# State space branch on one core: the bias difference of the decays and the scaling of the results on ScalarE, and the state step for four heads in one instruction

## The chip, the cores and the metric

The kernel runs on one core of a Trainium2 chip. The time is the device time of one execution in microseconds (us). The core's engines work side by side, each through its own list of instructions in order: TensorE (PE, matmuls and transposes; its weight loads are listed as PEld), VectorE (DVE), ScalarE (ACT), GpSimd (POOL, which here mostly issues transfers) and SyncE (SP, which issues transfers of weights). An engine waits when the next instruction in its own list needs something that is not there yet, and all that stands behind that instruction waits too.

## The reference

The kernel computes two transformer-like blocks on 512 tokens in fp32. The change lies in one branch of the second block, a state space branch: 8 groups of 4 heads, sequences cut in chunks of 128 tokens, run forwards and backwards. Cut to what matters:

```python
def segsum_exp(a):
    T = a.shape[-1]
    cs = jnp.cumsum(a, axis=-1)
    diff = cs[..., :, None] - cs[..., None, :]
    tri = jnp.asarray(np.tril(np.ones((T, T), dtype=bool)))
    return jnp.where(tri, jnp.exp(jnp.where(tri, diff, 0.0)), 0.0)

def ssd_chunked(x, dt, A, Bm, Cm):
    ...
    CB = jnp.einsum('bclgn,bcsgn->bcgls', Cc, Bc)
    Wd = CB[:, :, :, None] * segsum_exp(adt)
    y_diag = jnp.einsum('bcgrls,bcsgrp->bclgrp', Wd, xdt)
    ...
    def step(carry, inp):
        st, dec = inp
        return carry * dec[..., None, None] + st, carry
    ...

def ssd_branch(z, xbc, dt_raw, conv_w, conv_b, dt_bias, a_log, d_skip, norm_g):
    xbc = jax.nn.silu(depthwise_conv_centred(xbc, conv_w, conv_b))
    ...
    y_fwd = ssd_chunked(xs, dt[:, :, 0], A[0], Bm, Cm)
    y_bwd = fl(ssd_chunked(fl(xs), fl(dt[:, :, 1]), A[1], fl(Bm), fl(Cm)))
    y = y_fwd + y_bwd + d_skip[:, None] * xs
    y = y.reshape(b, l, D_INNER) * jax.nn.silu(z)
    yg = y.reshape(b, l, SSD_GROUPS, D_INNER // SSD_GROUPS)
    yg = yg * lax.rsqrt(jnp.mean(yg * yg, axis=-1, keepdims=True) + EPS)
    return yg.reshape(b, l, D_INNER) * norm_g
```

Three places of it are touched: the exponents inside `segsum_exp` (forward and backward decays of a chunk are put into one 128x128 matrix per head), `step`, and the product with the `rsqrt`.

## The kernel before, in words

All projections are fp32 products made of three PE passes: `mm3` (L457 to L459) multiplies high and low halves. A projection matmul is 128x128 by 128x512; eight input blocks times three passes, 24 matmuls, fill one of the three wide PSUM buffers (`psm`), which ACT and DVE then empty. Smaller results go through five buffers `pss`. A framework with a scheduler decides in which order each engine's instructions are listed: it plays the program through a timeline of its own and picks what it thinks is ready. So a change of a few lines can reorder the lists around it.

The state space stage works through groups g = 0 to 7. Its names and lines:

- `feats`: two projections of the next group, each emptied by `conv`: ACT L1253 (first tap, with bias) and DVE L1257 (four more taps, read from PSUM), then ACT L1259 (Silu). A `psm` buffer is free after both.
- `turn`: PE transposes the features (L1302, L1303), ACT copies them out (L1304, L1305).
- `first`: PE L1343 makes C·B (`cb`) for four chunks, DVE L1346 takes its diagonal, `step` makes the states (DVE L1310 weights x, PE L1312 multiplies, then ACT L1315 for the first chunk or DVE L1319 for the later ones), and `decays` makes the four 128x512 decay matrices of a group: a POOL transfer (L1327) brings the running sums of all four heads and both directions from DRAM (`aD`) to the 1024-word buffer `ab`, DVE L1329 adds the difference `dlt` of the two directions' biases to the backward half, DVE L1330 copies the forward half over it where the mask says so, ACT L1332 takes four Exp of 128x128 with a bias for each head, DVE L1333 multiplies by `cb`.
- `gate`: for even g, the gate projection with Silu on ACT (L1292).
- `second`: PE L1368/L1370 and DVE L1375/L1376 add the states' part, PE L1381 multiplies the decays by x, DVE L1382 and L1383 finish the chunk and ACT L1384 squares and sums it. L1384 is the last reader of that chunk's `ab`; there are four of them, so the next group's transfer of the same chunk follows it.
- `third`: DVE L510 and POOL L506 make the reciprocal root of the sum (`rr`), DVE L1392 scales the four chunks by it, PE L1394 transposes them, ACT L468 and DVE L469 split them into high and low.
- `ssd_out`: output projections, added up by ACT L623 and DVE L625.

Weights come through SP, and ACT L165 and DVE L167 split them into halves; these two run all the time. Exp, Silu and Ln need different function tables on ACT: an ACT_TABLE_LOAD stands in ACT's list wherever the table changes.

Of the kernel before, what the change touches and what calls it, by code (L numbers as in the profile page):

```python
# [12 lines left out]
AF = mybir.ActivationFunctionType  # L13
ALU = mybir.AluOpType
# [4 lines left out]
P = 128  # L19
# [38 lines left out]
def vw(ap, off, dims):  # L58

    return bass.AP(tensor=ap.tensor, offset=ap.offset + off, ap=[list(ap.ap[0])] + [list(x) for x in dims])  # L60


def dr(ap, off, dims):
    return bass.AP(tensor=ap.tensor, offset=ap.offset + off, ap=[list(x) for x in dims])
# [182 lines left out]
def body(ctx, tc, I, out, dbg=None, stop=None):  # L247
    nc = tc.nc
# [14 lines left out]
    def PS():  # L263
        return ps_s.tile([P, 512], F32, tag="s", name="pss")
# [125 lines left out]
    def colof(nm, k):  # L390
        c = col[nm] + k
        return COL[:, c:c + 1]
# [11 lines left out]
    ps = PS()  # L404
# [42 lines left out]
    def uk(k):  # L447
        if k < 4:
            return UAh[:, k], UAl[:, k]
        return st["UBh"][:, k - 4], st["UBl"][:, k - 4]  # L450
# [10 lines left out]
    def split(dst, src, scale=None):  # L461

        hi, lo = dst
        if scale is None:
            nc.scalar.activation(out=hi, in_=src, func=AF.Copy)  # L465
            nc.vector.tensor_tensor(out=lo, in0=src, in1=hi.bitcast(F32), op=ALU.subtract)  # L466
        else:
            nc.scalar.activation(out=hi, in_=src, func=AF.Copy, scale=scale)  # L468
            nc.vector.scalar_tensor_tensor(out=lo, in0=src, scalar=scale, in1=hi.bitcast(F32), op0=ALU.mult, op1=ALU.subtract)  # L469
# [39 lines left out]
    def rstd4(ss, n):  # L509
        nc.vector.tensor_scalar(out=ss, in0=ss, scalar1=1.0 / n, scalar2=EPS, op0=ALU.mult, op1=ALU.add)  # L510
        return inv_sqrt(ss, 4)
# [248 lines left out]
    o = 0  # L760
# [6 lines left out]
    ps = PS()  # L767
# [362 lines left out]
    for k in range(8 * NT + AHEAD + DELAY):  # L1130
# [3 lines left out]
        q = k - AHEAD - DELAY  # L1134
# [55 lines left out]
    def tok64(tag):  # L1190
        return wk.get(tag, 256).rearrange("p (c h) -> p c h", c=4)

    dtk, nb, dec, wst, ea = (tok64(n) for n in ("dtk", "nb", "dec", "wst", "ea"))
    dlt = wk.get("dlt", 128).rearrange("p (c h) -> p c h", c=4)
# [66 lines left out]
    def bc64(ap):  # L1261

        return vw(ap, 0, [list(ap.ap[1]), [0, 64]])

    h4 = lambda ap: ap.rearrange("p (h d) -> p h d", h=4)

    class Group:
# [39 lines left out]
        def step(s, di, c, prev):  # L1307
            xw = wk.get("xw", 256, 2)
            o = di * 32 + s.hs
            nc.vector.tensor_tensor(out=h4(xw), in0=h4(s.x[:, c]), in1=bc64(wst[:, c, o:o + 4]), op=ALU.mult)  # L1310
            ps = PS()
            nc.tensor.matmul(ps[:, 0:256], s.Bt[:, c], xw, start=True, stop=True)  # L1312
            S_ = wk.get(f"S{di}", 256, 3)
            if prev is None:
                nc.scalar.activation(out=S_, in_=ps[:, 0:256], func=AF.Copy)  # L1315
            else:
                for q in range(4):
                    sl = slice(q * 64, (q + 1) * 64)
                    nc.vector.scalar_tensor_tensor(out=S_[:, sl], in0=prev[:, sl], scalar=dec[:, c, o + q:o + q + 1],  # L1319
                                                   in1=ps[:, sl], op0=ALU.mult, op1=ALU.add)  # L1320
            return S_

        def decays(s, c):

            g, hs = s.g, s.hs
            ab = s.ab[c] = wk.get("ab", 1024, 4)
            nc.gpsimd.dma_start(ab.rearrange("p (d l) -> p d l", d=8), dr(aD, g * 8 * 512 + c * P, [[0, P], [512, 8], [1, P]]))  # L1327
            fw, T = h4(ab[:, 0:512]), h4(ab[:, 512:1024])
            nc.vector.tensor_tensor(out=T, in0=T, in1=vw(dlt[:, c, hs:hs + 4], 0, [[1, 4], [0, P]]), op=ALU.add)  # L1329
            nc.vector.copy_predicated(T, vw(masks, 7 * P, [[0, 4], [1, P]]), fw)  # L1330
            for q in range(4):
                nc.scalar.activation(out=T[:, q], in_=T[:, q], func=AF.Exp, bias=nb[:, c, hs + q:hs + q + 1])  # L1332
            nc.vector.tensor_tensor(out=T, in0=T, in1=vw(s.cb, c * P, [[0, 4], [1, P]]), op=ALU.mult)  # L1333
# [52 lines left out]
        def third(s):  # L1386

            z, g = s.z, s.g
            r = rstd4(s.ss, 256)
            pts = [PS(), PS()]  # L1390
            for c in range(4):
                nc.vector.tensor_scalar(out=z[:, c], in0=z[:, c], scalar1=r[:, c:c + 1], scalar2=None, op0=ALU.mult)  # L1392
                for n in range(2):
                    nc.tensor.transpose(pts[n][:, c * P:(c + 1) * P], z[:, c, n * P:(n + 1) * P], ident)  # L1394
            for n in range(2):
                split(uk((2 * g + n) % 4), pts[n], colof("ssd_norm_2", 2 * g + n))
# [302 lines left out]
```

## Time and profile before

| | us |
|---|---|
| time, median of 3 runs (lowest to highest) | 2580.79 (2578.79 to 2582.44) |
| time of the profiled execution | 2581.83 |
| its span in the profile | 2580.1 |
| PE busy in the span | 2504.9 |
| DVE busy | 1714.5 |
| ACT busy | 1220.2 |
| the state space stage, from 1340 to 1800 | 460.0 |

The span runs from the first to the last recorded instruction of the profiled execution. Busy time of different engines overlaps. The stage's boundaries are rounded to 20 us; its two ends also hold a little of the work before and after it.

### The profile page before, as it was taken

To read this page: it belongs to the slowest core of one execution; us is meant where nothing else is said; L and a number is where in the kernel's file an instruction comes from. 1 tells how busy PE (TensorE), PEld (TensorE's weight loads), DVE (VectorE), ACT (ScalarE), POOL (GpSimd) and SP (SyncE) were. 2 spreads that over 40 slices of the span, in tenths; PEclk is the share of its full clock that TensorE was granted. 3 is DMA by queue.
4 is the path that set the end of the run, shared out by engine and by line. 5 is a ranking of instruction groups with operands and counts; after the bars stand their busy time and mean duration, and the time that the engine had idled before them with its cause. 6 is when DMAs were issued, how large, how long until landed. Compare 5 with 4: busy or idle time off the path is not lost. (4 is left out here: it accounts for less than half of the span.)

```text
span 2580.1 us, 33650 instructions
## 1 busy us (share of the span) xinstructions
PE 2504.9 (97%) x12848; PEld 2088.2 (81%) x12848; DVE 1714.5 (66%) x3048; ACT 1220.2 (47%) x2181; POOL 183.5 (7%) x199
## 2 busy tenths in 40 slices
PE   8999999999999989999999999998999999999998
PEld 7888888778888768877888788787887789878877
DVE  5566567775566657577477788887555466487674
ACT  6333345443476554444356554563455436444342
POOL 1100220000201030000121100010000000100000
PEclk9999999999999989999999999998999999999999
DMA  5521235333232133453334333352221233243441
GB/s 175 162 66 61 87 115 169 125 108 129 82 96 89 63 97 113 140 179 98 102 109 125 106 104 109 104 148 77 73 67 40 84 113 123 82 147 104 141 139 58
DMA packets 202001, 278.11 MB, mean 108 GB/s; under 512 B 10800, under 2 KB 127776, under 8 KB 201840
## 3 DMA queue, kind: packets, MB, share of 16 engines
q1 hardware_dynamic: 190352, 236.29, 29.4%
q0 software_dynamic: 10192, 34.96, 5.0%
q10 hardware_dynamic: 1296, 4.72, 0.5%
q8 instruction: 101, 1.65, 0.3%
q14 instruction: 60, 0.49, 0.1%
HBM read 271.56 MB, written 9.61 MB: 109 GB/s over the span
## 5 line engine op out<-in xcount | busy, mean ns | idle before, releaser
L458 PE MATMUL psm<-XTl,hl 128*128 128x512 f32 (+1 forms) x1400 | 537.3, 384 | 7.8 <-DVE XTl L466 7.8
L457 PE MATMUL psm<-XTh,hl 128*128 128x512 f32 (+1 forms) x1400 | 534.5, 382 | 5.9 <-ACT XTh L465 5.1
L459 PE MATMUL psm<-XTh,hl 128*128 128x512 f32 (+1 forms) x1400 | 533.3, 382 | 0.0
L165 ACT ACTIVATE hl<-raw 128x1024 fp32r<-128x1024 f32 x303 | 319.3, 1056 | 313.9 <-PE psm L459 132.6
L167 DVE TENSOR_TENSOR hl<-raw,hl 128x1024 fp32r<-128x1024 f32 x287 | 352.7, 1233 | 149.0 <-ACT hl L165 147.9
L458 PEld LDWEIGHTS psm<-XTl,hl 128*128 128x128 f32 x1400 | 266.3, 190 | 56.9 <-DVE XTl L466 8.6
L457 PEld LDWEIGHTS psm<-XTh,hl 128*128 128x128 f32 x1400 | 265.9, 190 | 55.7 <-ACT XTh L465 6.1
L459 PEld LDWEIGHTS psm<-XTh,hl 128*128 128x128 f32 x1400 | 266.3, 190 | 48.5
L457 PE MATMUL psm<-hl,XTh 128*128 128x512 f32 (+1 forms) x640 | 231.1, 362 | 4.4 <-ACT XTh L465 3.3
L458 PE MATMUL psm<-hl,XTh 128*128 128x512 f32 (+1 forms) x640 | 229.9, 359 | 0.1
L459 PE MATMUL psm<-hl,XTl 128*128 128x512 f32 (+1 forms) x640 | 229.1, 358 | 0.0
L457 PE MATMUL psm<-hl,UAh 128*128 128x512 f32 x368 | 148.6, 405 | 4.9 <-DVE ACC L625 1.5
L458 PE MATMUL psm<-hl,UAh 128*128 128x512 f32 x368 | 144.9, 395 | 0.0
L459 PE MATMUL psm<-hl,UAl 128*128 128x512 f32 x368 | 143.7, 396 | 0.0
L457 PEld LDWEIGHTS psm<-hl,XTh 128*128 128x128 f32 x640 | 122.3, 191 | 21.8 <-ACT XTh L465 3.7
L458 PEld LDWEIGHTS psm<-hl,XTh 128*128 128x128 f32 x640 | 122.2, 191 | 16.6 <-issue 0.5
L459 PEld LDWEIGHTS psm<-hl,XTl 128*128 128x128 f32 x640 | 122.3, 191 | 15.9 <-issue 0.5
L671 ACT ACTIVATE WK<-psm 128x512 f32<-128x512 f32 x66 | 39.5, 598 | 160.8 <-PE psm L459 160.8
L457 PE MATMUL psm<-hl,UBh 128*128 128x512 f32 (+1 forms) x240 | 93.5, 391 | 1.1 <-ACT UBh L468 0.8
L459 PE MATMUL psm<-hl,UBl 128*128 128x512 f32 (+1 forms) x248 | 94.3, 388 | 0.0
L1257 DVE SCALAR_TENSOR_TENSOR WS<-psm,CW,WS 128x511 f32<-128x511 f32 (+1 forms) x120 | 87.5, 740 | 8.7 <-ACT WS L1253 8.4
L458 PE MATMUL psm<-hl,UBh 128*128 128x512 f32 (+1 forms) x240 | 92.2, 386 | 0.0
(481 smaller groups left out, 4839.2 us busy)
## 6 DMA issues: line engine op xcount, KB each, us to landing
raw<-in_mlp_w_down_dram SPq DMA_DIRECT2D x76, 512.0 KB, 3.3
raw<-in_mlp_w_up_dram SPq DMA_DIRECT2D x64, 512.0 KB, 3.9
raw<-in_w_in_dram SPq DMA_DIRECT2D x60, 512.0 KB, 3.7
raw<-in_w_down_dram SPq DMA_DIRECT2D x38, 512.0 KB, 3.9
WS<-aD POOLq DMA_DIRECT2D x32, 512.0 KB, 5.9
raw<-in_w_up_dram SPq DMA_DIRECT2D x32, 512.0 KB, 3.7
raw<-in_w_in_dram SPq DMA_DIRECT2D x33, 256.0 KB, 3.2
raw<-in_a_w_in_dram SPq DMA_DIRECT2D x16, 512.0 KB, 4.9
```

Of the source, the lines that this page charges most:

```text
L165: s.nc.scalar.activation(out=h, in_=r, func=AF.Copy)
L167: eng.tensor_tensor(out=l, in0=r, in1=h.bitcast(F32), op=ALU.subtract)
L457: nc.tensor.matmul(ps, a[0], b[0], start=first, stop=False, skip_group_check=partial)
L458: nc.tensor.matmul(ps, a[0], b[1], start=False, stop=False, skip_group_check=partial)
L459: nc.tensor.matmul(ps, a[1], b[0], start=False, stop=last, skip_group_check=partial)
L671: nc.scalar.activation(out=rl, in_=ps, func=AF.Relu)
L1257: nc.vector.scalar_tensor_tensor(out=dst[:, o0:o1], in0=ps[:, o0 + d:o1 + d], scalar=cw(j), in1=dst[:, o0:o1], op0=ALU.mult, op1=ALU.add)
```

## The change

Line numbers up to 1314 stay; behind the step they are smaller by one or two. In the changed kernel the step is L1317 and L1318, the transfer L1325, the bias difference L1328, the masked copy L1329, the Exp L1331, the diagonal of `cb` L1345, the values L1380 to L1382, the square L1383 and the scaling L1391.

- `step`, three states in four: four DVE instructions 128x64 that multiply the previous state by the head's decay and add the matmul's result (L1319) become one DVE multiplication 128x256 with the four decays broadcast (L1317, which does not read the matmul's result) and one DVE addition 128x256 from PSUM (L1318).
- `decays`: one DVE addition 128x512 (L1329) becomes four ACT Identity 128x128 (L1328), each with the head's difference as a bias per partition.
- `third`: four DVE scalings 128x256 (L1392) become four ACT Copy with the scale read per partition (L1391).

```diff
--- before.py
+++ after.py
@@ -1314,10 +1314,8 @@
             if prev is None:
                 nc.scalar.activation(out=S_, in_=ps[:, 0:256], func=AF.Copy)
             else:
-                for q in range(4):
-                    sl = slice(q * 64, (q + 1) * 64)
-                    nc.vector.scalar_tensor_tensor(out=S_[:, sl], in0=prev[:, sl], scalar=dec[:, c, o + q:o + q + 1],
-                                                   in1=ps[:, sl], op0=ALU.mult, op1=ALU.add)
+                nc.vector.tensor_tensor(out=h4(S_), in0=h4(prev), in1=bc64(dec[:, c, o:o + 4]), op=ALU.mult)
+                nc.vector.tensor_tensor(out=S_, in0=ps[:, 0:256], in1=S_, op=ALU.add)
             return S_
 
         def decays(s, c):
@@ -1326,7 +1324,8 @@
             ab = s.ab[c] = wk.get("ab", 1024, 4)
             nc.gpsimd.dma_start(ab.rearrange("p (d l) -> p d l", d=8), dr(aD, g * 8 * 512 + c * P, [[0, P], [512, 8], [1, P]]))
             fw, T = h4(ab[:, 0:512]), h4(ab[:, 512:1024])
-            nc.vector.tensor_tensor(out=T, in0=T, in1=vw(dlt[:, c, hs:hs + 4], 0, [[1, 4], [0, P]]), op=ALU.add)
+            for q in range(4):
+                nc.scalar.activation(out=T[:, q], in_=T[:, q], func=AF.Identity, bias=dlt[:, c, hs + q:hs + q + 1])
             nc.vector.copy_predicated(T, vw(masks, 7 * P, [[0, 4], [1, P]]), fw)
             for q in range(4):
                 nc.scalar.activation(out=T[:, q], in_=T[:, q], func=AF.Exp, bias=nb[:, c, hs + q:hs + q + 1])
@@ -1389,7 +1388,7 @@
             r = rstd4(s.ss, 256)
             pts = [PS(), PS()]
             for c in range(4):
-                nc.vector.tensor_scalar(out=z[:, c], in0=z[:, c], scalar1=r[:, c:c + 1], scalar2=None, op0=ALU.mult)
+                nc.scalar.activation(out=z[:, c], in_=z[:, c], func=AF.Copy, scale=r[:, c:c + 1])
                 for n in range(2):
                     nc.tensor.transpose(pts[n][:, c * P:(c + 1) * P], z[:, c, n * P:(n + 1) * P], ident)
             for n in range(2):
```

The scheduler's lists change with it inside the state space stage; POOL's and SP's lists keep their order. ACT's list holds 58 table loads after, 56 before. Three places follow.

ACT at the start of group 0, before, from the table load of L1234 (the end of the preparation of the decay biases) to L1245, an Exp of a `pss` buffer that DVE L1246 reads after it and that `cb` waits for:

```order
L1234 ACTIVATE WS<-WS 128x256
L1292 ACT_TABLE_LOAD
L1292 ACTIVATE h<-psm 128x512
L1332 ACT_TABLE_LOAD
L1332 ACTIVATE WS<-WS 128x128 x4
L165 ACTIVATE hl<-raw 128x1024
L1332 ACTIVATE WS<-WS 128x128 x7
L1245 ACTIVATE WS<-pss 128x256
```

The same place in the changed kernel:

```order
L1234 ACTIVATE WS<-WS 128x256
L1328 ACTIVATE WS<-WS 128x128 x8
L1292 ACT_TABLE_LOAD
L1292 ACTIVATE h<-psm 128x512
L1328 ACTIVATE WS<-WS 128x128 x4
L1331 ACT_TABLE_LOAD
L1331 ACTIVATE WS<-WS 128x128 x4
L165 ACTIVATE hl<-raw 128x1024
L1331 ACTIVATE WS<-WS 128x128 x4
L1245 ACTIVATE WS<-pss 128x256
```

Twelve Identities stand ahead of the Exps; the gate's L1292 stands behind eight of them, and L1245 behind all twelve.

ACT where group 3 gives way to group 4, before, from the first Exps of group 4 to the split L468 of group 3's results (the L1384 among them is the square of group 3's last chunk):

```order
L1332 ACTIVATE WS<-WS 128x128 x4
L1304 ACTIVATE WS<-pss 128x256
L1305 ACTIVATE WS<-pss 128x128
L1384 ACTIVATE WS,ss<-h 128x256
L1292 ACT_TABLE_LOAD
L1292 ACTIVATE h<-psm 128x512
L1332 ACT_TABLE_LOAD
L1332 ACTIVATE WS<-WS 128x128 x12
L1292 ACT_TABLE_LOAD
L1292 ACTIVATE h<-psm 128x512
L165 ACTIVATE hl<-raw 128x1024
L468 ACTIVATE UAh<-pss,COL 128x512 x2
```

The same place in the changed kernel, up to the scaling of group 3's results:

```order
L1331 ACT_TABLE_LOAD
L1331 ACTIVATE WS<-WS 128x128 x4
L1292 ACT_TABLE_LOAD
L1292 ACTIVATE h<-psm 128x512
L1383 ACTIVATE WS,ss<-h 128x256
L1328 ACTIVATE WS<-WS 128x128 x4
L1304 ACTIVATE WS<-pss 128x256
L1305 ACTIVATE WS<-pss 128x128
L1328 ACTIVATE WS<-WS 128x128 x4
L1331 ACT_TABLE_LOAD
L1331 ACTIVATE WS<-WS 128x128 x4
L1391 ACTIVATE h<-h,rr 128x256 x4
```

The square of the last chunk (now L1383) stands behind a table load, four Exps, another load and the gate's L1292; between it and the scaling L1391 stand eight Identities, two copies, a table load and four Exps.

DVE where group 1 gives way to group 2, before, from the scaling of group 1's results to the first weighting of x (L1310) that stands behind the diagonal of `cb` (listed as ISA):

```order
L1392 TENSOR_SCALAR h<-h,rr 128x256 x4
L167 TENSOR_TENSOR hl<-raw,hl 128x1024
L1329 TENSOR_TENSOR WS<-WS 128x512
L167 TENSOR_TENSOR hl<-raw,hl 128x1024
L1330 COPY_PREDICATED WS<-masks,WS 128x512
L1257 SCALAR_TENSOR_TENSOR WS<-psm,CW,WS 128x510
L1257 SCALAR_TENSOR_TENSOR WS<-psm,CW,WS 128x511 x2
L1346 ISA WS,cbd<-pss,ident 128x128
L1346 ISA cbd 128x1
L469 SCALAR_TENSOR_TENSOR UAl<-pss,COL,UAh 128x512
L1310 TENSOR_TENSOR WS<-WS 128x256
```

The same place in the changed kernel, from L510:

```order
L510 TENSOR_SCALAR ss<-ss 128x4
L1257 SCALAR_TENSOR_TENSOR WS<-psm,CW,WS 128x510
L1257 SCALAR_TENSOR_TENSOR WS<-psm,CW,WS 128x511
L1329 COPY_PREDICATED WS<-masks,WS 128x512
L1257 SCALAR_TENSOR_TENSOR WS<-psm,CW,WS 128x511
L1257 SCALAR_TENSOR_TENSOR WS<-psm,CW,WS 128x510
L1329 COPY_PREDICATED WS<-masks,WS 128x512
L167 TENSOR_TENSOR hl<-raw,hl 128x1024
L1329 COPY_PREDICATED WS<-masks,WS 128x512
L1345 ISA WS,cbd<-pss,ident 128x128
L1345 ISA cbd 128x1
L1310 TENSOR_TENSOR WS<-WS 128x256
```

The scaling and the additions of the bias difference are gone from DVE's list, and the convolution's L1257 have moved up; the masked copies (now L1329) stay.

Counted in projection matmuls (128x512) that PE's list holds ahead of it, the first L1343 of group 0 stands 5 later than before, and the first L1394 of group 0 19 later, of group 1 28 later and of group 3 15 later.

## Rows read from the trace of the kernel before

**Rows 1.** The page, part 1: busy time of each engine over the span.

```profile
PE 2504.9 (97%) x12848; PEld 2088.2 (81%) x12848; DVE 1714.5 (66%) x3048; ACT 1220.2 (47%) x2181; POOL 183.5 (7%) x199
```

**Rows 2.** Stretch 1340 to 1800 us: length, busy per engine, TensorE clock, DMA share, GB/s.

```profile
1340.00:1800.00 460.00, 436.80 (x2117) 363.77 (x2115) 367.75 (x826) 254.29 (x483) 41.81 (x46) 0.97 0.40 112
```

**Rows 3.** The same columns for one 20 us slice of that stretch.

```profile
1480.00:1500.00 20.00, 15.90 (x63) 12.47 (x62) 19.86 (x50) 11.01 (x17) 0.00 (x0) 0.91 0.27 79
```

**Rows 4.** Waits of PE in 1340 to 1800: total us, times, longest.

```profile
PE pss L1394 <- DVE h L1392: 8.1, 3, 4.5
PE pss L1312 <- DVE WS L1310: 3.8, 2, 2.9
PE pss L1381 <- DVE WS L1382: 3.3, 2, 2.4
PE psm L457 <- DVE WS L1257: 2.3, 2, 1.5
PE pss L1343 <- DVE WS L1246: 1.6, 1, 1.6
PE pss L1370 <- DVE WS L1319: 1.2, 1, 1.2
```

**Rows 5.** Groups of instructions in 1340 to 1800: busy us, mean ns, idle before.

```profile
L165 ACT ACTIVATE hl<-raw 128x1024 fp32r<-128x1024 f32 x59 | 62.0, 1056 | 34.7 <-PE psm L459 27.5 <-DMA raw<-in_w_ssd_branch_dram 7.2
...
L1332 ACT ACTIVATE WS<-WS 128x128 f32<-128x128 f32 x128 | 41.0, 391 | 13.2 <-DVE WS L1330 12.9
...
L1319 DVE SCALAR_TENSOR_TENSOR WS<-WS,pss 128x64 f32<-128x64 f32 x128 | 27.1, 272 | 0.0
...
L1332 ACT ACT_TABLE_LOAD x18 | 23.1, 1283 | 3.5 <-DMA WS<-aD 3.2
...
L1329 DVE TENSOR_TENSOR WS<-WS 128x512 f32<-128x512 f32 x32 | 22.0, 688 | 35.2 <-DMA WS<-aD 35.2
...
L1376 DVE TENSOR_TENSOR WS<-WS 128x256 f32<-128x256 f32 x48 | 18.6, 413 | 0.1
...
L1384 ACT ACTIVATE WS<-h 128x256 f32<-128x256 f32 x32 | 13.2, 414 | 36.5 <-DVE h L1383 36.5
...
L1392 DVE TENSOR_SCALAR h<-h,rr 128x256 f32<-128x256 f32 x32 | 9.1, 349 | 3.1 <-POOL rr L506 3.0
```

**Rows 6.** Waits of all engines, same stretch: DVE for the decay transfers.

```profile
DVE WS L1329 <- DMA WS<-aD: 35.2, 20, 3.4
```

**Rows 7.** Timeline at the first group's decays: start, length, engine, line, idle before.

```profile
1365.96 0.69 DVE L1329 TENSOR_TENSOR WS<-WS 128x512 f32<-128x512 f32 x1 [1.45 <-DMA WS<-aD]
...
1371.51 0.36 ACT L1245 ACTIVATE WS<-pss 128x256 f32<-128x256 f32 x1
...
1373.85 0.39 PE L457 MATMUL psm<-XTh,hl 128*128 128x512 f32 x1
...
1374.54 0.40 PE L457 MATMUL psm<-XTh,hl 128*128 128x512 f32 x1
```

**Rows 8.** Timeline where group 0 gives way to group 1.

```profile
1406.59 0.42 ACT L1384 ACTIVATE WS<-h 128x256 f32<-128x256 f32 x1 [0.83 <-DVE h L1383]
...
1412.83 0.69 DVE L1329 TENSOR_TENSOR WS<-WS 128x512 f32<-128x512 f32 x1 [1.93 <-DMA WS<-aD]
...
1416.54 0.76 ACT L1253 ACTIVATE WS<-psm,CW 128x512 f32<-128x512 f32 x1
```

**Rows 9.** Timeline of DVE where group 1 gives way to group 2.

```profile
1476.87 0.69 DVE L1329 TENSOR_TENSOR WS<-WS 128x512 f32<-128x512 f32 x1 [1.80 <-DMA WS<-aD]
```

**Rows 10.** Timeline where group 3 gives way to group 4.

```profile
1572.45 0.69 DVE L1329 TENSOR_TENSOR WS<-WS 128x512 f32<-128x512 f32 x1 [2.79 <-DMA WS<-aD]
...
1575.56 0.41 ACT L1384 ACTIVATE WS<-h 128x256 f32<-128x256 f32 x1
...
1577.37 0.60 ACT L1292 ACTIVATE h<-psm 128x512 f32<-128x512 f32 x1
...
1580.95 1.03 PE L1394 MATMUL pss<-ident,h 128*128 128x128 f32 x8
```

## The prediction

> **What bounds the kernel now.** I began with the page's busy times: PE works in 2504.9 of the 2580.1 us, so PE's list is the bound of the whole run and only its gaps can be won [rows 1]. Then I cut out the stretch in which every touched line lies. In 460 us PE works 436.80, so 23.2 us are gaps; DVE works 367.75 (80%) and ACT 254.29 (55%) [rows 2]. Third, the list of what PE waited for there: six rows, all released by DVE, add up to 8.1 + 3.8 + 3.3 + 2.3 + 1.6 + 1.2 = 20.3 us of those gaps [rows 4]. So DVE is late, in a few places, and each place has its own reason. One gap also costs clock: in the slice from 1480 the granted clock is 0.91 while PE stands 4.10 us; 9% of 15.90 busy us, 1.4 us, is my estimate of what that part at 1.2 GHz cost [rows 3]. Last I looked at what DVE itself waits for: 35.2 us in 20 waits for the decay transfers, up to 3.4 each, all at L1329 [rows 6]. The reader is to see that the instruction that moves is also the one at which DVE stands.
>
> **The change, part by part: engine time.** DVE loses the 32 additions, 22.0 us, and the 32 scalings, 9.1 [rows 5]. Its 128 small state updates (27.1 us) become 64 instructions of 128x256; at the 413 ns of L1376, the same shape, that is 26.4, a gain of 0.7 [rows 5]. The broadcast operand and the PSUM source could make one 0.35 to 0.45 us, so 22 to 29. DVE falls by about 32, from 368 to 336.
>
> ACT takes on 128 Identities with a bias. Nearest is L1332, the same shape and bias pointer with Exp: 41.0 us for 128, 0.32 each [rows 5]. From below an Identity might be 0.25 (32 us); from above it is the 391 ns of one alone (50). I take 41, since they come in fours as the Exps do. The 32 Copies of 128x256 I put at L1384's 13.2 us for the same number and shape [rows 5] (bounds 10 and 16, by the same shares). Two more table loads at 1.28 (23.1/18) are 2.6 [rows 5]. That Identity and Copy need no load of their own is seen in the order, where L1328 and L1391 stand behind Exp or ahead of Silu without one. ACT rises by 57, to 311 (68%); no engine's sum becomes the bound. Each chunk's chain to its Exps grows by 1.28 − 0.69 = 0.6 us and one handover.
>
> One chunk's addition costs 0.69 us on DVE and 1.28 on ACT, so 32 of them cost 19 us more engine time than before [rows 5]. The Trainium skill, "ScalarE: Activation LUTs", section "Rules for kernel authors", says that add and multiply belong on VectorE and not on ScalarE. The trace agrees on engine time, and by that rule the change would lose, at worst those 19 us if PE waited for all of them. But the engine that PE waits for here is DVE [rows 4], so the sum is made from the waits, place by place, and the loss stands among the rivals.
>
> **Place by place.** A PE step that keeps pace is one projection matmul in 0.23 us: three from 1373.85 to 1374.54 [rows 7].
>
> Start of group 0. L1343 waited 1.6 us for L1246, and that for L1245 [rows 4]. In the new order L1245 stands behind all the Identities. From the second chunk's landing at 1365.96 I add ACT's list: four Identities 1.28, load 1.28, L1292 0.60, four Identities 1.28, load 1.28, Exps 1.28, L165 1.06, Exps 1.28, together 9.3, so 1375.3 instead of 1371.51: 3.8 later [rows 5, 7, 10]. Five projection matmuls now ahead of L1343 cover 5 × 0.23 = 1.2. **+2.6** (bounds 0 and +3.8).
>
> Group 0 to 1. L1394's 4.5 us [rows 4] ends with DVE's scaling. Now ACT, free from about 1407, stands at the first Identity until the transfer lands at 1412.83 [rows 8], 5.7 us, with two squares, copies and L1253 behind it. From there: four Identities 1.28, two squares 0.83, six copies at most 0.41 each, L165 1.06, a load 1.28 and Exps 1.28, up to 8.2, so L1253 at 1420 to 1421 instead of 1416.54 [rows 5, 8]. L1394 stands 19 matmuls (4.4 us) later and no longer has to be waited for; but those matmuls need the PSUM buffer that L1253 frees, 3.5 to 4.5 late. The gap changes its name and I put it at 3.7. **−0.8** (bounds −4.5 and +3).
>
> Group 1 to 2. Here the step waits 2.9 for L1310, then 1.2 for L1319 [rows 4], and DVE had stood 1.80 for a transfer just before [rows 9]. In the new list no addition stands there, the convolution moves up, and PE comes 28 matmuls (6.4 us) later. Both gaps and the slice's 1.4 of clock go. **−5.5** (bounds 0 and −5.5).
>
> Group 3 to 4. ACT starts the first Identities at the landing, 1572.45 [rows 10]. Four Identities, seven copies and squares (about 2.0), a load, four Exps, a load and L1292 make 7.7, so the last square starts at 1580.2 instead of 1575.56 [rows 5, 10]. Square, eight Identities, two copies, a load and four Exps (6.2) put L1391 at 1586.4. PE had L1394 at 1580.95 without a wait, and has 15 more matmuls, so is there at 1584.4 [rows 10]. **+2.0** (bounds 0 and +4; the last L1310 gap of 0.9 stays).
>
> Elsewhere. The two waits on L1257, 2.3 us, are DVE's backlog in the convolution, which L1253 starts in time there: **−2.3** (bounds 0 and −2.3). Of the 3.3 us on L1382 at the stage's end DVE's relief is worth half, as the state updates are only 0.7 shorter in all: **−1.6**. Scaling then transposing at the end costs 0.41 instead of 0.35 before the first transpose can start and one handover: **+0.2**. Waits on ACT that I haven't followed, in the four other changes of group: **+1.0**.
>
> The sum is +2.6 − 0.8 − 5.5 + 2.0 − 2.3 − 1.6 + 0.2 + 1.0 = −4.4 us. On the profiled execution's own 2581.83 that is 2577.4; that execution was 1.04 above the median of 2580.79, so on the median it is **2576.4**, rounded to 2576.5.
>
> **Rivals.** Full relief: the waits on ACT fall where PE has cover, since PE's list was rearranged with the change. Then all DVE rows but L1343's (18.7) and the 1.4 of clock can go, 12 to 20 us: 2561 to 2569. For it: the 19, 28 and 15 matmuls put in front. Against: gaps are also release of PSUM buffers, which ACT now delays.
>
> Names only: DVE's gaps go and ACT's come at the same size, 2578 to 2584. For it speaks group 0 to 1.
>
> The other side: ACT's list, held at the transfer. DVE's 35.2 us of standing [rows 6] pass to an engine that has 57 us more to do. A square behind the held Identity is also what frees the next `ab` buffer, so the next transfer starts later too. There are seven changes of group; a hold of 5.7 us at each, with 2 to 3 us of it reaching PE through L1253, is 14 to 21, less the 9 that DVE's relief wins (5.5, 2.3 and 1.6): +5 to +12, 2586 to 2593. It decides from where L1253 or L1292 comes later than the two other `psm` buffers can be filled, 2 × 24 × 0.23 = 11 us. Against: ACT has 149 us free, and 12 of the 32 transfers landed before DVE came to them. Two table loads more are only 2.6 of it.
>
> The change not doing what it says: a multiplication for four heads that takes 0.8 instead of 0.41 us would leave DVE 25 us lighter instead of 32; this shifts no case.
>
> **How the numbers follow.** The forecast with its own range 2572 to 2580 has 0.41, names only 0.23, full relief 0.13, the other side 0.23. About 5.2 us, 0.2%, is what a measurement of this kernel can tell from no change: faster means under 2575.6. The forecast lies near that line: 0.26 of its 0.41 below it, and all of full relief, 0.39. Slower has the other side's 0.23 and 0.01 for what lies beyond all four, 0.24. The rest, 0.37, is the same. The range for 8 in 10 leaves out the lower half of full relief and the upper part of the other side: 2564 to 2591.
>
> **What would show it.** In the changed profile the stage should show DVE near 336 and ACT near 311, with L1328 at 41 and L1391 at 13. PE's waits on L1310, L1257 and the old scaling should be gone or under 3 us in all; L1343 should wait 3 to 5 us at group 0; L1394 should wait on ACT L1391 at the change from 3 to 4; ACT should stand some 30 us at L1328 for transfers. I am wrong if PE's waits on ACT in the stage pass 15 us (the other side), or if PE's gaps fall under 10 us (full relief), or if Identity costs more than 0.4 us in a row of four.

## The result: 1.0124 times as long, and the profile after

The changed kernel takes 2613.28 us (median of 4 runs, 2610.73 to 2616.07) beside 2581.61 for the kernel before (its three runs above and a fourth): a ratio of 1.0124, interval 1.0107 to 1.0142, about 32 us more. The prediction had 4 us less.

The page of the changed kernel, part 1, answers to [rows 1]:

```profile
PE 2517.2 (96%) x12848; PEld 2093.0 (80%) x12848; DVE 1685.1 (64%) x2920; ACT 1272.4 (49%) x2343; POOL 182.6 (7%) x199
```

The span is 2614.3, 34.2 more than before. Some 2 us of that lie ahead of the stage: ACT L1230, which stands ahead of everything that was changed, starts at 1358.58 instead of 1356.40. The stage itself ends near 1834 instead of 1800. Its busy times (columns as in [rows 2]) and five 20 us slices of it:

```profile
1340.00:1836.00 496.00, 451.77 (x2131) 370.18 (x2130) 342.02 (x702) 306.88 (x647) 40.42 (x46) 0.95 0.37 104
...
1500.00:1520.00 20.00, 15.35 (x70) 12.13 (x69) 17.25 (x38) 18.10 (x35) 0.00 (x0) 0.96 0.29 79
...
1540.00:1560.00 20.00, 20.00 (x102) 16.42 (x101) 8.05 (x13) 18.67 (x52) 3.68 (x4) 1.00 0.56 156
...
1600.00:1620.00 20.00, 17.30 (x75) 13.95 (x75) 5.73 (x11) 19.90 (x45) 1.92 (x2) 0.91 0.27 59
...
1620.00:1640.00 20.00, 16.55 (x72) 13.19 (x72) 20.00 (x44) 9.35 (x15) 0.00 (x0) 0.95 0.50 152
...
1760.00:1780.00 20.00, 15.70 (x76) 12.45 (x74) 12.84 (x19) 19.86 (x41) 2.81 (x3) 1.00 0.39 114
```

The engine sums came out as forecast: DVE 342 (336), ACT 307 (311). PE now stands 496 − 451.77 = 44.2 us instead of 23.2. The other part is clock: one minus the granted clock times PE's busy time, summed over the 20 us slices, is my estimate of the time lost at 1.2 GHz; it gives about 20 us after and 10 before. 21 us of gaps and 11 of clock are the 32 (the window is 36 us longer, since it also takes in the 2.2 us that lie ahead and runs 1.8 past the stage's end). The reader is to see the fourth busy figure in the slices: ACT works 18.10, 19.90 and 19.86 of 20 us, at places where one group gives way to the next. Over the stage it is 62% busy. A full slice of ACT alone does not make PE stand: from 1540 to 1560 ACT works 18.67 us and PE all 20.00; and from 1620 to 1640 PE stands 3.45 us while DVE, not ACT, is the full one.

What PE waited for in the changed kernel's stage (answers to [rows 4]):

```profile
PE psm L457 <- DVE WS L1257: 9.5, 4, 3.5
PE pss L1393 <- ACT h L1391: 6.8, 3, 3.5
PE pss L1342 <- ACT WS L1305: 4.0, 1, 4.0
PE pss L1369 <- DVE WS L1318: 3.4, 1, 3.4
PE pss L1380 <- DVE WS L1381: 3.2, 2, 1.9
PE pss L1312 <- DVE WS L1310: 3.0, 4, 1.7
PE pss L1312 <- ACT WS L1315: 2.8, 2, 1.7
PE psm L457 <- ACT h L1292: 2.7, 1, 2.7
PE pss L1303 <- ACT WS L1259: 2.4, 1, 2.4
```

No row is large. ACT, for which PE waited 1.6 us in all before, stands in five of these nine with 18.7 us, and L1257's row has grown from 2.3 to 9.5. The waits of the other engines in the same stretch show what DVE and ACT themselves stood for (answers to [rows 6]):

```profile
DVE WS L1329 <- ACT WS L1328: 56.2, 26, 9.1
...
ACT WS L1328 <- DMA WS<-aD: 30.1, 10, 6.1
...
DVE WS L1257 <- ACT WS L1253: 11.1, 8, 2.4
```

DVE no longer stands 35.2 us for transfers; it stands 56.2 for ACT's Identities. ACT stands 30.1 for the transfers, and then has four Identities to do. The groups of new work on ACT, and the Exps beside them (answers to [rows 5]; busy us, mean ns, idle before):

```profile
L1328 ACT ACTIVATE WS<-WS 128x128 f32<-128x128 f32 x128 | 41.7, 393 | 33.4 <-DMA WS<-aD 30.1 <-PE psm L459 3.1
...
L1331 ACT ACTIVATE WS<-WS 128x128 f32<-128x128 f32 x128 | 41.3, 395 | 1.0 <-DVE WS L1329 0.8
...
L1391 ACT ACTIVATE h<-h,rr 128x256 f32<-128x256 f32 x32 | 13.6, 497 | 1.4 <-POOL rr L506 1.4
```

Their cost is what was forecast, 41 and 13; the idle time ahead of L1328 is the hold.

The timeline of ACT, PE and DVE where group 3 gives way to group 4 (answers to [rows 10]), from the last square:

```profile
1602.94 0.41 ACT L1383 ACTIVATE WS<-h 128x256 f32<-128x256 f32 x1
...
1603.34 1.27 ACT L1328 ACTIVATE WS<-WS 128x128 f32<-128x128 f32 x4
...
1604.94 1.28 ACT L1328 ACTIVATE WS<-WS 128x128 f32<-128x128 f32 x4
1606.23 1.28 ACT L1331 ACT_TABLE_LOAD   x1
1607.53 1.28 ACT L1331 ACTIVATE WS<-WS 128x128 f32<-128x128 f32 x4
1608.71 1.69 ACT L1391 ACTIVATE h<-h,rr 128x256 f32<-128x256 f32 x4
...
1609.26 1.83 PE L1393 MATMUL pss<-ident,h 128*128 128x128 f32 x8 [2.70 <-ACT h L1391]
...
1615.09 0.97 ACT L1328 ACTIVATE WS<-WS 128x128 f32<-128x128 f32 x3
...
1616.09 0.76 DVE L1329 COPY_PREDICATED WS<-masks,WS 128x512 f32<-128x512 uint8 x1 [9.11 <-ACT WS L1328]
...
1636.37 0.70 PE L1369 MATMUL pss<-WS 128*128 128x256 f32 x2 [3.45 <-DVE WS L1318]
```

ACT works here without a pause. L1391 starts 5.8 us after the last square (6.2 forecast), and PE waits 2.70 for it. DVE stands 9.11 us for the last Identities, which stand behind the scaling in ACT's list; from 1620 to 1640 DVE then works all 20 us, and PE stands 3.45 for L1318. So the walk at this place was right as far as it went; it ended at L1391, and the trace shows DVE's lateness reaching PE once more behind it; how much of the 3.45 comes of those 9.11 was not tested apart.

### The profile page after: what moved, and what is told of

It reads as the page before. It is cut to its first block, busy times and chain, and to the rows that moved or that the text cites. A ratio compares the mean times of both kernels' runs of the same rounds, so it can differ in the third digit from the quotient of the medians.

```text
span 2614.3 us, 33665 instructions
## 1 busy us (share of the span) xinstructions
PE 2517.2 (96%) x12848; PEld 2093.0 (80%) x12848; DVE 1685.1 (64%) x2920; ACT 1272.4 (49%) x2343; POOL 182.6 (7%) x199
## 5 line engine op out<-in xcount | busy, mean ns | idle before, releaser
L1257 DVE SCALAR_TENSOR_TENSOR WS<-psm,CW,WS 128x510 f32<-128x510 f32 (+1 forms) x120 | 88.1, 745 | 19.4 <-ACT WS L1253 18.8
```

The lines of the kernel that those rows point to most:

```text
L1257: nc.vector.scalar_tensor_tensor(out=dst[:, o0:o1], in0=ps[:, o0 + d:o1 + d], scalar=cw(j), in1=dst[:, o0:o1], op0=ALU.mult, op1=ALU.add)
```

## The experiments

All ratios are against runs of the kernel before on the same chip; times in us are the ratio's difference on 2583.

**Each part alone, in lists that the scheduler makes for it.** The first takes only the second piece of the diff, the second only the third, the third only the first; the fourth takes the first and third.

> Only the bias difference goes to ACT; step and scaling as before. Theory H (hold): ACT stands at the first Identity of a chunk until the decay transfer lands (30.1 us in 10 waits in the changed kernel), and squares, copies, L1253 and L1292 behind it come late; then nearly the whole loss is here, +20 to +32 us against before. Theory L (load): ACT has 42 us more to do here, three quarters of the 56 us it got in all; then +20 to +26. Theory O (order): the lists of the whole stage come out worse by chance; then anything from -10 to +30, and parts without Identity are as bad.

> Only the scaling L1392 goes to ACT. H: no transfer stands in ACT's list, so -4 to +3 us against before. L: 13.6 us more on ACT, a quarter of the load, +6 to +10. O: anything between -10 and +20.

> Only the state step for four heads at once. H and L: ACT's work is unchanged and DVE has about 1 us less to do, -4 to +3 us against before. O: the lists change too, anything between -10 and +20. A rival on this part alone: the wait of PE on L1318 (3.4 us once in the changed kernel, 1.2 before) is the price of the split step; then +2 to +4.

> The change without the Identities (step and scaling changed, bias difference on DVE). H: -6 to +4 us against before, so some 30 under the changed kernel. L: +6 to +10. O: anything.

| | ratio | interval | us |
|---|---|---|---|
| Identities alone | 1.0097 | 1.0082 to 1.0112 | +25 |
| scaling alone | 1.0044 | 1.0032 to 1.0057 | +11 |
| step alone | 1.0013 | 1.0004 to 1.0022 | +3 |
| step and scaling | 1.0015 | 1.0006 to 1.0023 | +4 |

The Identities carry most of it. But scaling alone costs 11 (above H's range and just above L's) and, with the step, the two cost 4 (inside H's, under L's), so the parts don't add up, and the order theory stayed alive.

**Hold or load, in own lists.** Two edits of the kernel before, each ahead of or behind a line of `decays`:

```diff
+            nc.scalar.activation(out=T[:, 0, 0:1], in_=T[:, 0, 0:1], func=AF.Copy)
             nc.vector.tensor_tensor(out=T, in0=T, in1=vw(dlt[:, c, hs:hs + 4], 0, [[1, 4], [0, P]]), op=ALU.add)
```

> The kernel before with one ACT copy of a single column (128x1) of each chunk's backward decays ahead of DVE's addition, so that ACT's list, too, stands until the transfer has landed; some 6 us more work for ACT, spread over 32 places. H: the hold alone costs most of what the Identities cost, +12 to +26 us against before. L: 6 of 42 us of load, +0 to +5. O: anything from -10 to +20, with no relation to ACT's waits for transfers.

```diff
             nc.vector.copy_predicated(T, vw(masks, 7 * P, [[0, 4], [1, P]]), fw)
+            for q in range(4):
+                nc.scalar.activation(out=T[:, q], in_=T[:, q], func=AF.Copy)
```

> The kernel before with four more ACT copies of 128x128 per chunk behind the masked copy and ahead of the Exps: 41 us more work for ACT, but what stands for the transfer is still DVE. H: the load alone is mostly hidden in ACT's 206 free us of the stage, 0 to +8 us against before. L: +20 to +30, as with the Identities.

The hold alone: 1.0051 (1.0036 to 1.0066), +13. The load alone: 1.0100 (1.0085 to 1.0115), +26. H expected 0 to 8 of the load; it falls as the only cause. L expected 0 to 5 of the hold; it falls as the only cause too. Since the copies of the second edit also lie on the chain from landing to Exp, the two can't be added up. Nor were these copies the forecast 41 us of work: 128 of them took 29.2, 0.23 each.

**More buffers for the transfers**, on the changed kernel (six needed the diagonal's scratch to move to an idle place):

```diff
-            ab = s.ab[c] = wk.get("ab", 1024, 4)
+            ab = s.ab[c] = wk.get("ab", 1024, 5)
```

> The changed kernel with five buffers for the decay transfers instead of four, so that a group's first transfer starts before the group ahead has squared its first chunk. H: the longest holds (5.9 us in front of a group's first chunk) go, -5 to -15 us against the changed kernel, 2598 to 2608. L: at most -3.

> The changed kernel with six buffers for the decay transfers (the scratch of the diagonal moves to an idle place to make room). H: two chunks land early, ACT's 30 us of waits for transfers fall under 12, -8 to -22 us against the changed kernel, 2591 to 2605. L: at most -4.

1.0149 (1.0132 to 1.0166) and 1.0142 (1.0127 to 1.0158): no faster. They decide nothing about the hold, since it did not go: ACT stood 38.3 and 33.8 us for the transfers, against 30.1. The scheduler put the Identities earlier in ACT's list: at the change from group 0 to 1, for one, all four of the first chunk stand ahead of the second square, where in the changed kernel two of them stand behind it.

**Instructions and lists apart.** Each engine's list can be pinned: behind the traced program, an edge that orders without waiting is drawn from each instruction to the one that is to follow it on its engine.

```python
    _by = {i.name: i for i in tc.nc.cur_bb.bb.instructions}
    for _l in _o:
...
        for _d in _l:
...
            if _q is not None:
                tc.add_manual_dep(_n, _q.name, _dep, reason="order")
            _q = _n
```

So new instructions can run in the old lists and old ones in the new lists.

> The changed kernel's instructions in the lists of the kernel before, pinned instruction by instruction on all five engines: each of the four Identities and each Copy stands in ACT's list where, by the trace of before, ACT was when DVE began the addition or scaling that it replaces. Theory O (order): the loss comes from the lists that the scheduler made for the change, so with the old lists it goes: -8 to +6 us against before. Theory R (resource: 57 us more work and the holds on ACT): it stays, +18 to +35.

> The counterpart: the instructions of the kernel before in the lists of the changed kernel, DVE's additions and scalings put where, by the trace of the changed kernel, DVE was when ACT began the Identity or Copy. O: +18 to +35 us against before. R: -5 to +8.

> Only the bias difference on ACT, in the pinned lists of the kernel before. O: -6 to +5 us against before, 20 to 30 under the same part with its own lists. R: +15 to +30.

> Step for four heads and scaling on ACT, bias difference left on DVE, in the pinned lists of the kernel before. O: -5 to +1 us against before. R: +2 to +8, as with its own lists (+4).

In three of these kernels scalings that share a place in a list stood in reverse order of the chunks, while PE waits for the first chunk first; with the Identities alone only two chunks of group 0 were swapped. The two with all of the instructions were mended and run again:

> The changed kernel's instructions in the pinned lists of the kernel before once more, the four scalings of a group and the Identities of two chunks that meet at one place now in the order of the chunks (in the first trial they stood in reverse, and PE waits for the first scaling first). If ACT's work and holds are the cause, +25 to +37 us against before, under the first trial's +41 and no better than the change with its own lists (+32). If the reverse order had been the cause of the first trial's loss: -6 to +6.

> The instructions of the kernel before in the pinned lists of the changed kernel, likewise mended. The first trial gave 0.9984 of before; with the scalings in order up to 1 us at each of eight places more can go: 0.996 to 0.999 of before, a version that beats both kernels. If the first trial was chance: 1.000 to 1.002.

| | old lists | new lists |
|---|---|---|
| old instructions | 1 | 0.9960 (0.9948 to 0.9973); reversed 0.9984 (0.9975 to 0.9993) |
| new instructions | 1.0133 (1.0117 to 1.0148); reversed 1.0160 (1.0145 to 1.0175) | 1.0124 (1.0107 to 1.0142) |

In the old lists the new instructions cost 34 us, in the new ones 32 + 10 = 42. Order is not the cause. The new lists are the better ones: with the old instructions they win 10 us, a version faster than both kernels. Pinning by itself costs nothing that shows: the trial with the load in ACT's pauses, further down, is pinned in the old lists too and stands at 0.9999. Identities alone in the old lists: 1.0095 (1.0080 to 1.0110), +25, as with own lists. Step and scaling in the old lists, reversed: 1.0034 (1.0023 to 1.0045), +9; how much of it the reversal is was not run.

What PE waited for in the fastest version, old instructions in the new lists:

```profile
PE psm L457 <- DVE WS L1257: 5.4, 4, 3.1
PE pss L1381 <- DVE WS L1382: 3.8, 2, 2.1
PE pss L1394 <- DVE h L1392: 3.6, 2, 3.4
```

L1394's wait is 3.6 instead of 8.1 [rows 4], and L1310 and L1319 are gone: the waits that the 19, 28 and 15 matmuls of the new list were to cover do go, for the old instructions.

**Hold, load and place, in the old lists.** The first is the one-column copy again, pinned where the Identities stood. The second puts four Identities there that read a constant and write a scratch; the third puts the same ones into ACT's 32 longest pauses.

```diff
+            jz = wk.get("jz", 512)
+            for q in range(4):
+                nc.scalar.activation(out=jz[:, q * P:(q + 1) * P], in_=ident, func=AF.Identity, bias=dlt[:, c, hs + q:hs + q + 1])
             nc.vector.tensor_tensor(out=T, in0=T, in1=vw(dlt[:, c, hs:hs + 4], 0, [[1, 4], [0, P]]), op=ALU.add)
```

> The kernel before in its own lists, pinned, with one ACT copy of a single column of each chunk's backward decays where the Identities stood in the pinned trials: ACT's list stands until the transfer has landed, for some 6 us of work. Theory hold: +12 to +22 us against before. Theory time (ACT's work at the changes of group): 0 to +6.

> The same pinned lists with four extra Identities of 128x128 at each of those 32 places that read a constant and write a scratch nobody reads: 41 us of ACT work, no wait for a transfer, no longer chain. Theory time: +10 to +22 us against before. Theory hold: -2 to +3. A third theory, that the chain from landing to Exp being longer costs it: -2 to +3 too.

> The same extra 128 Identities, each four of them put into one of the 32 longest pauses that ACT had in the stage in the trace of before (1.9 to 7.6 us each). If the place decides, -2 to +5 us against before; if the sum of ACT's work decides, as much as with the extra Identities at the decays.

| old lists, pinned | ratio | interval | us |
|---|---|---|---|
| hold at the decays | 1.0053 | 1.0038 to 1.0068 | +14 |
| load at the decays | 1.0051 | 1.0036 to 1.0066 | +13 |
| load in ACT's pauses | 0.9999 | 0.9989 to 1.0008 | 0 |
| Identities (both) | 1.0095 | 1.0080 to 1.0110 | +25 |

14 and 13 are 27, and the Identities cost 25 (interval 21 to 28): the two halves are enough to account for it. That they simply add is not shown, since the Identities also take 22 us of additions off DVE, which the two halves leave there. Nor is the hold's price the time that ACT stands for transfers: that is 14.7 us here and was 47.3 for the same edit in its own lists, at 14 and 13 us. The stage's busy times with the load at the decays (columns as in [rows 2]):

```profile
1340.00:1800.00 460.00, 430.35 (x2083) 358.04 (x2081) 362.10 (x809) 287.76 (x602) 39.27 (x43) 0.98 0.39 109
```

and with the load in ACT's pauses:

```profile
1340.00:1800.00 460.00, 435.06 (x2113) 362.32 (x2112) 367.98 (x826) 291.75 (x611) 41.52 (x46) 0.97 0.40 112
```

ACT does 288 us of work in the one and 292 in the other; PE works 4.7 us less in the first by 1800, and ends later still. PE's longest waits in the first:

```profile
PE pss L1312 <- DVE WS L1310: 10.3, 3, 3.8
PE pss L1397 <- DVE h L1395: 9.2, 3, 4.8
```

and the same two rows in the second:

```profile
PE pss L1397 <- DVE h L1395: 8.8, 3, 4.8
...
PE pss L1312 <- DVE WS L1310: 3.3, 3, 2.1
```

The wait of the step for L1310 was 3.8 before [rows 4]; it is 3.3 with the load in the pauses and 10.3 with the load at the decays. It is DVE that PE waits for in both, and the lists of every engine but ACT are the same in both: what DVE needs from ACT comes later at the changes. DVE's own waits at L1310, for ACT's copies of the features, show it; at the decays:

```profile
DVE WS L1310 <- ACT WS L1304: 5.9, 4, 2.6
```

and in the pauses:

```profile
DVE WS L1310 <- ACT WS L1304: 1.8, 2, 1.5
```

**The reverse**, on the kernel before, with its own lists:

```diff
-                nc.scalar.activation(out=t2, in_=s.z[:, c], func=AF.Square, accum_out=s.ss[:, c:c + 1])
+                nc.vector.tensor_tensor_reduce(out=t2, in0=s.z[:, c], in1=s.z[:, c], scale=1.0, scalar=0.0, op0=ALU.mult,
+                                               op1=ALU.add, accum_out=s.ss[:, c:c + 1])
```

> The reverse of the change on the kernel before, with lists of its own: the squares with their sum (19.3 us on ACT) go to DVE as one multiply-and-add-up instruction each, about 0.42 us, 13 to 16 us. Theory time: ACT is relieved at the changes of group and a handover goes, -10 to -2 us against before. If DVE's backlog is dearer, as the prediction had it: +3 to +10.

1.0047 (1.0030 to 1.0064), +12, above both ranges and against theory time's. Taking 19 us off ACT and giving 16 to DVE costs as well: PE's wait for DVE's scaling is 15.1 instead of 8.1, so at the changes DVE has no room either, as the prediction had it. The lists are the scheduler's own here, so their part in the 12 is not held apart.

## Why the prediction was wrong, by its own steps

The step that failed is that ACT's free time would hide the new work, so that DVE's relief (−5.5, −2.3 and −1.6) could be taken as won. None of the three came as a gain: PE's gaps grew by 21 us where the sum had them shrink by 3, and the clock, which the sum had only as −1.4, cost 10.5 more. By place (gaps are the length less PE's busy time; the clock is estimated from the 20 us slices as above; L1257's −2.3 and L1382's −1.6 are put where those waits lay):

| place | before, us | after, us | gaps | clock | forecast, both |
|---|---|---|---|---|---|
| start of group 0 | 1340 to 1400 | 1340 to 1400 | +5.4 | +1.8 | +1.8 |
| group 0 to 1 | 1400 to 1460 | 1400 to 1460 | +1.7 | +4.3 | −0.8 |
| group 1 to 2 | 1460 to 1520 | 1460 to 1540 | +3.2 | +2.0 | −5.5 |
| group 3 to 4 | 1560 to 1600 | 1580 to 1640 | +5.2 | +2.4 | +2.0 |
| the four other changes | between | between | +4.2 | +0.6 | −0.5 |
| the end | 1780 to 1800 | 1800 to 1836 | +1.3 | −0.5 | −1.4 |

The four places that were walked through lost 26 of the 32. Their rows before (columns as in [rows 2]):

```profile
1340.00:1400.00 60.00, 57.62 (x274) 46.62 (x273) 43.38 (x93) 42.85 (x69) 4.78 (x6) 1.00 0.43 117
1400.00:1460.00 60.00, 55.49 (x279) 47.27 (x278) 50.15 (x122) 28.48 (x61) 5.70 (x7) 0.94 0.32 92
1460.00:1520.00 60.00, 55.90 (x273) 46.82 (x272) 48.55 (x105) 36.49 (x71) 7.07 (x7) 0.97 0.47 127
...
1560.00:1600.00 40.00, 39.06 (x196) 32.77 (x195) 28.96 (x70) 24.60 (x52) 4.61 (x5) 1.00 0.41 115
```

and after:

```profile
1340.00:1400.00 60.00, 52.20 (x241) 41.04 (x239) 33.75 (x67) 44.13 (x82) 4.78 (x6) 0.96 0.39 110
1400.00:1460.00 60.00, 53.84 (x237) 43.87 (x238) 46.45 (x97) 39.60 (x82) 4.58 (x5) 0.87 0.35 97
1460.00:1540.00 80.00, 72.71 (x345) 59.91 (x345) 52.86 (x111) 41.90 (x93) 5.55 (x6) 0.95 0.31 87
...
1580.00:1640.00 60.00, 53.85 (x257) 44.51 (x256) 40.22 (x87) 36.55 (x78) 4.61 (x5) 0.95 0.40 106
```

- **Engine time** was right: L1328 41.7 (41), L1391 13.6 (13.2), DVE 342 (336), ACT 307 (311). "No engine's sum becomes the bound" is true of the sums, and what was concluded from it failed. In the pinned trials 41 us of extra work cost nothing in ACT's pauses and 13 us at the decays. The 149 free microseconds were an average over the stage. The new work, 4 × 1.28 + 1.7 = 6.8 us a group, lands at the changes, ahead of squares, copies and Exps that DVE and PE wait for. In the slices there ACT had 2 to 9 us of 20 free before; in six of them it now works 18 to 20. How full a slice was before did not tell by itself where the loss would come: the fullest, ACT at 18.04 us from 1680 to 1700, lies at a change (5 to 6) that lost 2.2 us.

```profile
1680.00:1700.00 20.00, 20.00 (x103) 16.99 (x102) 14.28 (x33) 18.04 (x38) 5.12 (x6) 1.00 0.53 158
```

- **Start of group 0**, +2.6: L1342 waited 4.0 instead of 1.6, so +2.4 in wait; right. L1245 started at 1377.30, or 3.6 later once the 2.2 ahead of the stage are taken off (3.8 forecast); the profile names L1305, which starts 0.5 us behind it in ACT's list, as the last releaser. The walk ended there, and PE stood 2.9 us more for L1257 before 1400.
- **Group 0 to 1**, −0.8: the walk was right, and its price was not. ACT stood 5.92 us at the first Identity (5.7 forecast), and L1394's wait went. PE stood 1.84 for L1257 and 2.66 for L1292 instead, 4.5 us for `psm` buffers (3.7 forecast), and 1.66 for ACT L1315, which was not on the walk. The clock's +4.3 was in no term.
- **Group 1 to 2**, −5.5: wrong. The waits for L1310 and L1319 went there, as forecast, but PE stood 1.95 for ACT L1305, 1.10 for ACT L1315, 3.55 for DVE L1257 and 0.69 for ACT L623 in their place: 7.3 us of gaps instead of 4.1.
- **Group 3 to 4**, +2.0: 2.70 waited; right up to L1391. The 3.45 for L1318 that followed, through DVE's 9.11 us of standing, was not in the walk.
- **L1257**, −2.3: wrong, 9.5 instead of 2.3. **L1382**, −1.6: wrong, 3.2 instead of 3.3. These steps counted DVE's relief and not that DVE would stand 56.2 us for ACT instead of 35.2 for transfers. Moving the instruction at which DVE stands did not remove the standing.
- **Clock**, −1.4: the prediction read one slice. Before, three of them had lost some 10 us together, most of it in the slice below (2.6) and at the stage's end (0.57 granted from 1780 to 1800, 5.5 us). After, twice as much was lost.

```profile
1420.00:1440.00 20.00, 15.49 (x66) 12.92 (x65) 15.17 (x33) 13.12 (x25) 1.05 (x1) 0.83 0.30 78
```

- **Waits not followed**, +1.0: too small, as the four other changes lost 4.8, but not the largest miss.
- **The other side**, 0.23, was the right rival in its mechanism and mis-sized: +5 to +12 against +32. It put a price on the hold and none on the load; the trials give them 14 and 13. It also counted DVE's relief against them, which did not come. The sign that the prediction had set for it came true: PE's waits on ACT pass 15 us, 18.7 in the rows above alone.
- The rule that stood against the change, of the Trainium skill, "ScalarE: Activation LUTs", "Rules for kernel authors" (add and multiply belong on VectorE), gave the right sign: the Identities alone cost 25 us. By the pinned trials the engine time alone is not the reason, since as many Identities that read a constant cost 13 us at the decays and nothing in ACT's pauses; and the squares, moved to VectorE, cost 12.
- **Full relief** was refuted for this change, but the new lists it counted on are worth something: 10 us with the old instructions in them.

What stays open: the price of the scaling by itself, which was +11 alone, and within +4 for both with the step; whether the decays' chain being one handover longer has a part of its own in the hold's 14; and why the hold costs the same with 14.7 and with 47.3 us of ACT standing for transfers.

## What to carry to other kernels

Before work is moved to an engine that is "half idle", cut the stage into slices as long as one step of its pipeline, read how much time the engine has free in those slices where the work will stand, and set the new work against it; the average says nothing about them. A slice that fills up is a warning and no proof: follow what stands behind the new work, on the other engines too and past the first wait, and count the clock that each new gap costs. An instruction that waits for a transfer takes its wait along: ask what stands behind it in the new list. And keep the lists apart from the instructions: pinning the order cost nothing that shows here and told within two runs that the scheduler was not to blame.

## What the runs showed of the hardware

Identities of 128x128 in fours cost the same 0.32 us each as Exps (41.7 and 41.3 us for 128), and no table load of their own stands ahead of them in ACT's list. Copies of 128x128 in fours, without a bias, cost 0.23 each (29.2 us for 128, in the trial with copies behind the masked copy); whether the bias or the function makes the difference was not run. Four Copies of 128x256 with a scale per partition from SBUF take 1.69 us together, 0.42 each, although the mean of one alone is 497 ns.
